# A two-block transformer on one core: row gathers of large expert units issued right behind their places, and two weight tiles of the first small experts loaded one step later

## The chip, the cores and the metric

The kernel runs on one core of a Trainium2 chip. The metric is the device time of one execution in microseconds (us); lower is better. The engines are named as in the profile: PE (matrix products; PEld its weight loads), DVE, ACT, POOL, and SP, which here only issues transfers. Transfers by DMA are started by SP (all weights) or by POOL (gathers of rows).

## The reference, cut to what matters

Four attention layers and a second block run first; the change lies in the last part, a mixture of experts over 256 tokens of width 1024 with 64 experts, 8 of which each token uses.

```python
def moe_ffn(h, w_router, e_bias, w_eg, w_eu, w_ed, w_sg, w_su, w_sd):
    ...
    gates = jnp.sum(jax.nn.one_hot(eidx, N_EXPERTS, dtype=jnp.float32) * w[..., None], axis=-2)
    ...
    def expert_chunk(args):
        xc, gch = args
        hg = jnp.einsum('cd,edf->cef', xc, w_eg)
        hu = jnp.einsum('cd,edf->cef', xc, w_eu)
        a = jax.nn.silu(hg) * hu * gch[..., None]
        return jnp.einsum('cef,efd->cd', a, w_ed)
    ...
    shared = (jax.nn.silu(t @ w_sg) * (t @ w_su)) @ w_sd
    return (routed + shared).reshape(B, S, D)
```

## The kernel before, in words

The kernel computes each expert only for the tokens that chose it. After routing, an expert with more than 64 tokens is a **large unit** (up to 128 tokens), two others share a step as a **small pair** (up to 64 tokens each). Units are numbered u = 0, 1, 2, ..., pairs p = 0, 1, .... `lone(u)` computes one large unit alone, for u = 0 to 4; then `both(5)`, `both(6)`, ... each compute one large unit and one small pair (pair p = u - 5), in a chain of branches that ends when the work does. `both(5)` is the first common step. From here on the order of instructions on each engine is the order in which the code is written; nothing is rescheduled.

A large unit needs three weight matrices (gate, up, down) of 1 MB each. SP loads them into the three raw buffers `eraw`, in halves or whole (`load(u, j, h)`); ACT rounds a half to its high part (`hi`, tile `ehi`) and DVE subtracts to get the low part (`lo`, tile `elo`). PE multiplies with high and low parts: `wide(u, a, 0)` gate, `wide(u, a, 1)` up, `down(u, hf)` down. A raw half can be loaded again only when `lo` has read it. A small pair needs six tiles of 1 MB, `pair0` to `pair5` (gate, up, down of both experts), and PE uses them without splitting (`wide_p`, `down_p`; tiles 4 and 5 are read by `down_p` at the end of a common step). `load_p(p, *js)` loads those tiles. The table `early` says in which lone unit which tiles of pair 0 are loaded.

The rows of a unit's tokens come by these steps. `onehot(u)` (on POOL, tile `pm`) and `onehot_p(p)` (POOL, tile `ps`) make 0/1 matrices of which token has which place. `places(u)` lets PE multiply them, and DVE copies the resulting token numbers to `ix` (L1896). `fetch(t, i)` (L1901, POOL) gathers 128 rows of 4 KB from `hrow` in device memory by those numbers, into `xr` for a large unit and into the single buffer `xrp` for a pair (numbers `ip`). `cols(u, j)` turns the rows on PE (L1908) and ACT and DVE split the result into `x` (L278, L279); `cols_p(j)` does the same for a pair without splitting. `cols(u + 1, ...)` runs in step u, so that a unit's rows must be there one step ahead.

In the kernel before, `fetch` of unit u + 1 stands at the start of step u, though `places(u + 1)` was written in step u - 1; between the two, on POOL, stand the one-hots at the end of step u - 1: `onehot(u + 3)`, and from lone(2) on those of a pair. The fetch of pair 0 stands at the start of lone(4).

Of the kernel before, what the change touches and what calls it, by code (L numbers as in the profile page):

```python
# [232 lines left out]
class Kernel:  # L233
# [1574 lines left out]
    def weights(self, col, j):  # L1808
        e = self.nc.sync.value_load(self.eid[0:1, col:col + 1], min_val=0, max_val=E - 1)
        return self.ins["w_exp"][bass.ds(e, 1), :, 2048 * j:2048 * j + 2048].rearrange("o p n -> p (o n)")  # L1810
# [6 lines left out]
    def load(self, u, j, h=None):  # L1817

        part = (lambda t: t) if h is None else lambda t: self.half(t, j, h)
        self.nc.sync.dma_start(part(self.eraw[j]), part(self.weights(u, j)))  # L1820
# [21 lines left out]
    def units(self, num, y):  # L1842
# [18 lines left out]
        xr = [mp.tile([P, D], F32, name=f"xr{i}") for i in range(2)]  # L1861
        xr_p = mp.tile([P, D], F32, name="xrp")
        self.yt = [xr[hf][:, tt * 512:(tt + 1) * 512] for hf in range(2) for tt in range(2)]
        ix, ix_p = [[mp.tile([P, 1], I32, name=f"{t}{i}") for i in range(2)] for t in ("ix", "ip")]
# [10 lines left out]
        def hi(j, h):  # L1875
            nc.scalar.activation(half(hl[0][j], j, h), half(raw[j], j, h), AF.Copy)  # L1876

        def lo(j, h):
            V.tensor_tensor(half(hl[1][j], j, h), half(raw[j], j, h), half(hl[0][j], j, h).bitcast(F32), OP.subtract)  # L1879
# [7 lines left out]
        def places(u):  # L1887

            t = pm[u // 2 % 2][:, :, u % 2]
            b = self.tbank()  # L1890
            for tt in range(2):
                nc.tensor.transpose(b[:, tt * P:(tt + 1) * P], t[:, tt].bitcast(F32), self.ident)
            for tt in range(2):
                nc.tensor.matmul(b[:, S:S + 4], t[:, tt], self.gsp[:, tt, u, :], start=(tt == 0), stop=(tt == 1))
            if u > 1:
                V.tensor_copy(ix[u % 2], b[:, S + 2:S + 3])  # L1896
            V.tensor_copy(pt[u % 4], b[:, :S])
            V.tensor_reduce(gc[u % 4], b[:, S:S + 2], AX.X, OP.add)

        def fetch(t, i):  # L1900
            nc.gpsimd.indirect_dma_start(out=t, out_offset=None, in_=self.hrow,  # L1901
                                         in_offset=bass.IndirectOffsetOnAxis(ap=i[:, :1], axis=0))
# [8 lines left out]
        def cols(u, j):  # L1911
            x = [t[:, 4 * j:4 * j + 4, (u % 2) * P:(u % 2 + 1) * P] for t in self.x]
            self.split(x[0], x[1], turned(xr[u % 2], j))

        def wide(u, a, c):
            ww = w(c, KT)
            for k in range(KT):
                x = [t[:, k, (u % 2) * P:(u % 2 + 1) * P] for t in self.x]
                for j, (q, p) in enumerate(((0, 0), (0, 1), (1, 0))):
                    nc.tensor.matmul(a[:, c * 256:(c + 1) * 256], x[p], ww[q][:, k, :],  # L1920
                                     start=(k == 0 and j == 0), stop=(k == KT - 1 and j == 2))

        def turn():
            b = self.tbank()
            for f in range(2):
                nc.tensor.transpose(b[:, f * P:(f + 1) * P], av[:, f * P:(f + 1) * P], self.ident)
            self.split(at[0], at[1], b[:, :S].rearrange("p (f t) -> p f t", f=2))
# [5 lines left out]
        def down(u, hf):  # L1933
            d = w(2, 2)
            a = self.abank()
            c = slice(512 * hf, 512 * hf + 512)
            for f in range(2):
                for j, (q, p) in enumerate(((0, 0), (0, 1), (1, 0))):
                    nc.tensor.matmul(a, at[p][:, f, :], d[q][:, f, c], start=(f == 0 and j == 0), stop=(f == 1 and j == 2))
            out(gc[u % 4], a, c)  # L1940

        def combine(t, hf):
            for tt in range(2):
                for p in range(2):
                    nc.tensor.matmul(y[tt][hf], t[:, tt * P:(tt + 1) * P], yo[p][:, 512 * hf:512 * hf + 512],  # L1945
                                     start=False, stop=False, skip_group_check=True)


        def load_p(p, *js):
            for j in js:  # L1950
                nc.sync.dma_start(R[j], weights(NB + 2 * p + j % 2, j // 2))
# [23 lines left out]
        def cols_p(j):  # L1975
            self.copy(xs[:, 4 * j:4 * j + 4, :], turned(xr_p, j), "va"[j])
# [21 lines left out]
                                     start=(f == 0), stop=(f == 1))  # L1998
            out(gc_p[p % 3], a, c)

        early = {1: (0,), 2: (1, 2), 3: (3,), 4: (4, 5)}

        def lone(u):


            if u:
                fetch(xr[(u + 1) % 2], ix[(u + 1) % 2])
            if u == L - 1:
                fetch(xr_p, ix_p[0])
            load(u + 1, 1, 0)  # L2010
            lo(1, 1)
            load(u + 1, 1, 1)
            if u:
                for h in range(2):
                    hi(2, h)
                    lo(2, h)
                    load(u, 2, h)
            load_p(0, *early.get(u, ()))
            a = self.abank()
            wide(u, a, 0)  # L2020
            if u:
                turn()
            else:
                places(2)
            if u > 1:
                combine(pt[(u - 2) % 4], 0)
            for h in range(2):
                hi(0, h)
                lo(0, h)
                load(u + 2, 0, h)  # L2030
            wide(u, a, 1)
            if u:
                cols(u + 1, 0)
            else:
                places(0)
            if u > 1:
                combine(pt[(u - 2) % 4], 1)
            nc.scalar.activation(sv, a[:, 0:256], AF.Silu)
            V.tensor_tensor(av, a[:, 256:512], sv, OP.mult)
            hi(1, 0)  # L2040
            if u:
                down(u - 1, 0)
                cols(u + 1, 1)
            places(u + 2 if u else 1)
            lo(1, 0)
            hi(1, 1)
            if u == L - 1:
                cols_p(0)
            if u:
                down(u - 1, 1)  # L2050
            if u == L - 1:
                cols_p(1)
            if u > L - 3:
                places_p(u - L + 2)
            onehot(u + 4)
            if u >= L - 3:
                onehot_p(u - L + 3)
# [8 lines left out]
        def both(u):  # L2066

            p = u - L
            fetch(xr[(u + 1) % 2], ix[(u + 1) % 2])
            fetch(xr_p, ix_p[(p + 1) % 2])  # L2070
            if not p:
                load(u + 1, 1, 0)
                lo(1, 1)
                load(u + 1, 1, 1)
                for h in range(2):
                    hi(2, h)
                    lo(2, h)
                    load(u, 2, h)
                turn()
                for hf in range(2):  # L2080
                    combine(pt[(u - 2) % 4], hf)
                for hf in range(2):
                    down(u - 1, hf)
            a = self.abank()
            wide(u, a, 0)
            if p:
                cut(u)
            nc.scalar.activation(sv, a[:, 0:256], AF.Silu)
            if not p:
                for hf in range(2):  # L2090
                    combine(pt[(u - 1) % 4], hf)
            places(u + 2)
            b = self.abank()
            wide_p(b, 0)
            load_p(p + 1, 0, 1)
            for h in range(2):
                hi(0, h)
                lo(0, h)
            load(u + 2, 0)
            cols(u + 1, 0)  # L2100
            nc.scalar.activation(sv_p, b[:, 0:256], AF.Silu)
            wide(u, a, 1)
            V.tensor_tensor(av, a[:, 256:512], sv, OP.mult)
            cols(u + 1, 1)
            if not p:
                cut(u)
            wide_p(b, 1, range(0, 4))
            turn()
            wide_p(b, 1, range(4, KT))
            load_p(p + 1, 2, 3)  # L2110
            V.tensor_tensor(av_p, b[:, 256:512], sv_p, OP.mult)
            hi(1, 0)
            lo(1, 0)
            down(u, 0)
            turn_p()
            hi(1, 1)
            lo(1, 1)
            load(u + 2, 1)
            down(u, 1)
            cols_p(0)  # L2120
            combine(pt[u % 4], 0)
            down_p(p, 0)
            combine(pt[u % 4], 1)
            down_p(p, 1)
            load_p(p + 1, 4, 5)
            cols_p(1)
            combine(pt_p[p % 3], 0)
            places_p(p + 2)
            combine(pt_p[p % 3], 1)
            onehot(u + 4)  # L2130
            onehot_p(p + 3)
# [74 lines left out]
```

## Time and profile before

| what | value |
|---|---|
| median of 3 runs | 1279.52 us (1278.63 to 1283.08) |
| the profiled execution's own time | 1282.81 us |
| its span, first to last instruction | 1280.9 us |
| mean granted PE clock | 0.977 of full speed |
| PE busy | 1206.8 us, 94% of the span |
| DVE, ACT, POOL busy | 960.9, 691.3, 239.1 us |
| transfers | 298.77 MB, mean 233 GB/s |

The span is 1.9 us shorter than the execution's own time, and that execution took 3.3 us more than the median. The work on the experts starts at about 892 us of the span. lone(0) runs to about 899 us; the first waiting matrix products of later steps are at 908 us in lone(1), 921 us in lone(2) and 935 us in lone(3); lone(4) runs from 940.5 us, both(5) from 956 us on, and the products end at about 1267 us. A row of a timeline gives start, duration, engine, line, operation, tiles written and read, shape and count, and in brackets how long the engine had been idle and what ended that.

### The profile page before, as it was taken

To read this page: it belongs to the slowest core of one execution; us is meant where nothing else is said; L and a number is where in the kernel's file an instruction comes from. 1 tells how busy PE (TensorE), PEld (TensorE's weight loads), DVE (VectorE), ACT (ScalarE), POOL (GpSimd) and SP (SyncE) were. 2 spreads that over 40 slices of the span, in tenths; PEclk is the share of its full clock that TensorE was granted. 3 is DMA by queue.
4 is the path that set the end of the run, shared out by engine and by line. 5 is a ranking of instruction groups with operands and counts; after the bars stand their busy time and mean duration, and the time that the engine had idled before them with its cause. 6 is when DMAs were issued, how large, how long until landed. Compare 5 with 4: busy or idle time off the path is not lost. (4 is left out here: it accounts for less than half of the span.)

```text
span 1280.9 us, 23092 instructions
## 1 busy us (share of the span) xinstructions
PE 1206.8 (94%) x8278; PEld 1021.1 (80%) x8278; DVE 960.9 (75%) x2395; ACT 691.3 (54%) x1508; POOL 239.1 (19%) x307
## 2 busy tenths in 40 slices
PE   5999998999989999999989999988889999999995
PEld 5887786998879987999879898777877777766773
DVE  6877889879987797878689679887884555555554
ACT  5667786446644564557755555543753443444431
POOL 2034521001100110001100000020551332222320
PEclk9988999999989999999999999999999999999998
DMA  7460314673357644777435225243998999999997
GB/s 292 150 258 13 111 43 148 246 264 130 107 197 272 231 150 167 264 265 261 172 141 181 100 95 197 101 170 136 370 401 307 400 380 388 388 398 385 375 391 284
DMA packets 50926, 298.77 MB, mean 233 GB/s; under 512 B 5776, under 2 KB 6576, under 8 KB 20848
## 3 DMA queue, kind: packets, MB, share of 16 engines
q1 hardware_dynamic: 42912, 271.94, 56.2%
q0 software_dynamic: 5728, 21.73, 4.8%
q10 hardware_dynamic: 2160, 3.52, 0.8%
q8 instruction: 67, 1.10, 0.4%
q14 instruction: 59, 0.48, 0.1%
HBM read 295.05 MB, written 2.11 MB: 232 GB/s over the span
## 5 line engine op out<-in xcount | busy, mean ns | idle before, releaser
L351 ACT ACTIVATE hi<-raw 128x512 fp32r<-128x512 f32 (+4 forms) x452 | 247.1, 604 | 128.2 <-PE acc L415 61.0
L358 DVE TENSOR_TENSOR lo<-raw,hi 128x512 fp32r<-128x512 f32 (+5 forms) x446 | 286.6, 670 | 27.7 <-ACT hi L351 26.7
L415 PE MATMUL acc<-x,hi 128*128 128x256 f32 x1440 | 278.3, 292 | 0.0
L415 PEld LDWEIGHTS acc<-x,hi 128*128 128x128 f32 x1440 | 229.1, 195 | 9.7 <-issue 7.9
L415 PE MATMUL acc<-x,lo 128*128 128x256 f32 x720 | 207.2, 288 | 3.1 <-DVE lo L358 3.1
L415 PEld LDWEIGHTS acc<-x,lo 128*128 128x128 f32 x720 | 140.1, 195 | 4.4 <-DVE lo L358 3.7
L1879 DVE TENSOR_TENSOR elo<-eraw,ehi 128x1024 fp32r<-128x1024 f32 x100 | 119.7, 1226 | 15.6 <-ACT ehi L1876 15.5
L453 PE MATMUL acc<-hi,x 128*128 128x256 f32 x544 | 108.5, 296 | 4.4 <-DVE x L279 1.9
L1876 ACT ACTIVATE ehi<-eraw 128x1024 fp32r<-128x1024 f32 x100 | 102.4, 1054 | 12.5 <-DMA eraw<-in_w_exp_dram 12.3
L1920 PE MATMUL acc<-ehi,x 128*128 128x256 f32 x512 | 94.8, 285 | 1.3 <-ACT x L273 1.3
L453 PEld LDWEIGHTS acc<-hi,x 128*128 128x128 f32 x544 | 89.9, 200 | 7.1 <-DVE x L279 3.0
L1982 PE MATMUL acc<-pair,xs 128*64 128x256 f32 x704 | 83.3, 384 | 0.0
L1920 PEld LDWEIGHTS acc<-ehi,x 128*128 128x128 f32 x512 | 80.4, 191 | 3.6 <-ACT x L273 1.5
L453 PE MATMUL acc<-lo,x 128*128 128x256 f32 x272 | 79.2, 292 | 0.3 <-DVE lo L358 0.3
L642 ACT ACTIVATE p<-sb,m 128x256 f32<-128x256 f32 (+1 forms) x136 | 61.2, 452 | 30.6 <-DVE m L641 26.0
L1920 PE MATMUL acc<-elo,x 128*128 128x256 f32 x256 | 72.6, 284 | 0.7 <-DVE elo L1879 0.7
L387 DVE SCALAR_TENSOR_TENSOR macc<-raw,sc,macc 128x512 f32<-128x512 f32 x84 | 63.5, 756 | 8.5 <-DMA raw<-in_w_all_dram 6.9
L278 ACT ACTIVATE x<-t 128x512 fp32r<-128x512 f32 x50 | 29.6, 596 | 70.5 <-PE t L1908 57.2
L1982 PEld LDWEIGHTS acc<-pair,xs 128*64 128x64 f32 x704 | 47.7, 137 | 24.4 <-issue 3.7
L583 PE MATMUL acc<-hi,g 128*128 128x512 f32 x192 | 63.1, 400 | 0.0
L1901 POOL DMA_INDIRECT xrp<-hrow,ip x12 | 19.9, 1659 | 200.8 <-PE o L1945 196.0
L453 PEld LDWEIGHTS acc<-lo,x 128*128 128x128 f32 x272 | 54.3, 200 | 0.5 <-DVE lo L358 0.5
(589 smaller groups left out, 2644.9 us busy)
## 6 DMA issues: line engine op xcount, KB each, us to landing
raw<-in_w_all_dram SPq DMA_DIRECT2D x128, 1024.0 KB, 4.8
pair<-in_w_exp_dram SPq DMA_DIRECT2D x72, 1024.0 KB, 8.0
eraw<-in_w_exp_dram SPq DMA_DIRECT2D x33, 1024.0 KB, 8.5
eraw<-in_w_exp_dram SPq DMA_DIRECT2D x40, 512.0 KB, 6.7
gain<-in_rows_dram POOLq DMA_DIRECT2D x8, 512.0 KB, 4.0
raw<-in_w_all_dram SPq DMA_DIRECT2D x2, 832.0 KB, 4.5
nab<-in_na_bias_dram POOLq DMA_DIRECT2D x1, 1536.0 KB, 7.1
h<-in_x_dram SPq DMA_DIRECT2D x2, 512.0 KB, 10.4
```

The lines of the kernel that those rows point to most:

```text
L278: self.cut = self.nc.scalar.activation(hi, src, AF.Copy)
L351: self.nc.scalar.activation(hi[:, c], raw[:, c], AF.Copy)
L358: eng.tensor_tensor(lo[:, c], raw[:, c], hi[:, c].bitcast(F32), OP.subtract)
L387: nc.vector.scalar_tensor_tensor(self.macc, w[:, k, :], sc, self.macc, op0=OP.mult, op1=OP.add)
L415: self.nc.tensor.matmul(av[:, i, :], w[:, k, c], x[u][:, k, :], start=(k == 0 and j == 0), stop=(k == nk - 1 and j == 2))
L453: self.nc.tensor.matmul(a[:, :n], self.x[u][:, k, tt * P:(tt + 1) * P], ww[:, k, :], start=(k == 0 and j == 0), stop=(k == KT - 1 and j == 2))
L583: self.nc.tensor.matmul(a, gt[u][:, 4 * i + k, tt * P:(tt + 1) * P], ww[:, k, :], start=(i == 0 and k == 0 and j == 0), stop=(i == 1 and k ...
L642: nc.scalar.activation(out, sb[:, :n], AF.Exp, bias=m, scale=-1.0, accum_out=ssum)
L1876: nc.scalar.activation(half(hl[0][j], j, h), half(raw[j], j, h), AF.Copy)
L1879: V.tensor_tensor(half(hl[1][j], j, h), half(raw[j], j, h), half(hl[0][j], j, h).bitcast(F32), OP.subtract)
L1920: nc.tensor.matmul(a[:, c * 256:(c + 1) * 256], x[p], ww[q][:, k, :], start=(k == 0 and j == 0), stop=(k == KT - 1 and j == 2))
L1982: nc.tensor.matmul(a[64 * e:64 * e + 64, c * 256:(c + 1) * 256], xs[:, k, 64 * e:64 * e + 64], t[e][:, k, :], start=(k == 0), stop=(k == K ...
```

## The change

In `places(u)`, for u > 1, the gather of the unit's rows is now issued as soon as DVE has been given the copy of the token numbers; the two fetches of large units at the start of `lone` and `both` are gone. Unit 2 is therefore fetched in lone(0), units 3 to 6 in lone(1) to lone(4), and every common step u fetches unit u + 2 in place of u + 1. Pair fetches stay where they were. The table `early` gives one tile of pair 0 to each of lone(1) to lone(4), and tiles 4 and 5 are loaded in both(5), behind the reload of the down weights. There is one gather more in all.

```diff
@@ -1896,6 +1896,8 @@
                 V.tensor_copy(ix[u % 2], b[:, S + 2:S + 3])
             V.tensor_copy(pt[u % 4], b[:, :S])
             V.tensor_reduce(gc[u % 4], b[:, S:S + 2], AX.X, OP.add)
+            if u > 1:
+                fetch(xr[u % 2], ix[u % 2])
...
-        early = {1: (0,), 2: (1, 2), 3: (3,), 4: (4, 5)}
+        early = {1: (0,), 2: (1,), 3: (2,), 4: (3,)}
 
         def lone(u):
 
 
-            if u:
-                fetch(xr[(u + 1) % 2], ix[(u + 1) % 2])
             if u == L - 1:
                 fetch(xr_p, ix_p[0])
             load(u + 1, 1, 0)
@@ -2066,7 +2066,6 @@
         def both(u):
 
             p = u - L
-            fetch(xr[(u + 1) % 2], ix[(u + 1) % 2])
             fetch(xr_p, ix_p[(p + 1) % 2])
             if not p:
                 load(u + 1, 1, 0)
@@ -2076,6 +2075,7 @@
                     hi(2, h)
                     lo(2, h)
                     load(u, 2, h)
+                load_p(0, 4, 5)
                 turn()
```

On POOL the order before, from lone(2) to the start of both(5), is this: `xr_10799` and `xr_10800` are the two buffers of large units (here units 4, 5, 6), `pm` the one-hots of units 6, 7, 8, `ps` those of pairs 0, 1, 2.

```order
129 L1825 TENSOR_SCALAR pm<-consts_e,place 128x128 x2
130 L1957 TENSOR_SCALAR ps_10310<-consts_e,place 128x64 x4
131 L1901 DMA xr_10799<-hrow,ix_10802 128x1024
132 L1825 TENSOR_SCALAR pm<-consts_e,place 128x128 x2
133 L1957 TENSOR_SCALAR ps_10311<-consts_e,place 128x64 x4
134 L1901 DMA xr_10800<-hrow,ix_10803 128x1024
135 L1901 DMA xrp<-hrow,ip_10804 128x1024
136 L1825 TENSOR_SCALAR pm<-consts_e,place 128x128 x2
137 L1957 TENSOR_SCALAR ps_10310<-consts_e,place 128x64 x4
138 L1901 DMA xr_10799<-hrow,ix_10802 128x1024
```

After the change the same stretch of POOL reads as follows (the lines of the new file are two higher).

```order
129 L1903 DMA xr_10799<-hrow,ix_10802 128x1024
130 L1825 TENSOR_SCALAR pm<-consts_e,place 128x128 x2
131 L1959 TENSOR_SCALAR ps_10310<-consts_e,place 128x64 x4
132 L1903 DMA xr_10800<-hrow,ix_10803 128x1024
133 L1825 TENSOR_SCALAR pm<-consts_e,place 128x128 x2
134 L1959 TENSOR_SCALAR ps_10311<-consts_e,place 128x64 x4
135 L1903 DMA xrp<-hrow,ip_10804 128x1024
136 L1903 DMA xr_10799<-hrow,ix_10802 128x1024
```

The gather of unit 5 has moved ahead of the six one-hots of unit 7 and pair 1, and the gather of pair 0 (`xrp`, `ip_10804`), which stood right behind it, now stands behind those six one-hots.

On SP this is the piece of lone(4), behind the reload of the halves of unit 4's down weights; each load is preceded by the reading of an expert's number.

```order
 L1809 ISA x2
-L1951 ISA
-L1951 DMA pair_10778<-in_w_exp_dram 128x2048
-L1809 TENSOR_LOAD eid
-L1809 ISA x2
-L1951 ISA
-L1951 DMA pair_10779<-in_w_exp_dram 128x2048
+L1953 ISA
+L1953 DMA pair_10777<-in_w_exp_dram 128x2048
```

Two tiles of pair 0 (`pair_10778`, `pair_10779`, its tiles 4 and 5) have left lone(4), and one tile (3) has come; those two now stand in both(5). In lone(2) two tiles have become one in the same way.

## Rows read from the trace of the kernel before

**Rows 1.** Windows: PE, PEld, DVE, ACT, POOL busy us, PE clock, DMA share, GB/s.
```profile
920.00:940.00 20.00, 17.30 (x110) 15.14 (x110) 14.96 (x23) 13.88 (x19) 7.86 (x9) 1.00 1.03 408
960.00:964.00 4.00, 3.21 (x8) 2.59 (x9) 0.73 (x2) 0.61 (x1) 3.04 (x6) 0.57 1.02 403
968.00:972.00 4.00, 4.00 (x31) 3.00 (x31) 1.71 (x5) 2.28 (x3) 1.02 (x1) 1.00 0.03 9
1020.00:1040.00 20.00, 20.00 (x155) 15.77 (x154) 10.80 (x21) 8.80 (x14) 7.72 (x8) 1.00 0.97 373
```

**Rows 2.** Waits, 880 to 980 us: who waited for whom, total us, times, longest us.
```profile
POOL xr L1901 <- DVE ix L1896: 28.2, 5, 7.7
PE t L1908 <- DMA xr<-hrow,ix: 4.1, 3, 1.6
```

**Rows 3.** Timeline of PE: rows turned, first products of both(5), use of pair tiles.
```profile
908.12 0.66 PE L1908 MATMUL t<-consts,xr 128*128 128x128 f32 x4 [1.26 <-DMA xr<-hrow,ix]
...
921.10 0.66 PE L1908 MATMUL t<-consts,xr 128*128 128x128 f32 x4 [1.21 <-DMA xr<-hrow,ix]
...
934.83 0.66 PE L1908 MATMUL t<-consts,xr 128*128 128x128 f32 x4 [1.61 <-DMA xr<-hrow,ix]
...
952.62 0.66 PE L1908 MATMUL t<-consts,xrp 128*128 128x128 f32 x4 [1.45 <-DVE ix L1896]
...
960.79 0.79 PE L1939 MATMUL acc<-ehi,at 128*128 128x512 f32 x1 [2.18 <-DVE at L279]
...
986.44 1.94 PE L1997 MATMUL acc<-pair,ats 128*64 128x512 f32 x8
```

**Rows 4.** Timeline of POOL: gathers (L1901) and one-hots (L1825 units, L1957 pairs).
```profile
902.10 1.07 POOL L1901 DMA_INDIRECT xr<-hrow,ix  x1 [0.17 <-DVE gc L1898]
...
915.94 5.35 POOL L1957 TENSOR_SCALAR ps<-consts_e,place 128x64 fp32r<-128x64 f32 x4
926.58 1.02 POOL L1901 DMA_INDIRECT xr<-hrow,ix  x1 [5.29 <-DVE ix L1896]
927.62 1.28 POOL L1825 TENSOR_SCALAR pm<-consts_e,place 128x128 fp32r<-128x128 f32 x2
928.89 4.29 POOL L1957 TENSOR_SCALAR ps<-consts_e,place 128x64 fp32r<-128x64 f32 x4
940.32 1.02 POOL L1901 DMA_INDIRECT xr<-hrow,ix  x1 [7.14 <-DVE ix L1896]
942.81 0.93 POOL L1901 DMA_INDIRECT xrp<-hrow,ip  x1 [1.47 <-DVE ip L1971]
...
1001.28 1.02 POOL L1901 DMA_INDIRECT xr<-hrow,ix  x1 [0.15 <-issue]
```

**Rows 5.** Timeline of DVE: token numbers, second split of rows, low parts.
```profile
895.88 0.16 DVE L1896 CAST ix<-t 128x1 int32<-128x1 f32 x1 [0.17 <-PE t L1894]
...
909.94 0.68 DVE L279 TENSOR_TENSOR x<-t,x 128x512 fp32r<-128x512 f32 x1
...
928.42 3.63 DVE L1879 TENSOR_TENSOR elo<-eraw,ehi 128x1024 fp32r<-128x1024 f32 x3
...
951.88 0.68 DVE L279 TENSOR_TENSOR x<-t,x 128x512 fp32r<-128x512 f32 x1
```

**Rows 6.** Tile xr, windows 912:925, 925:938, 939:948: gathers from issue to landing.
```profile
DMA to landing us min/median/max: 7.4/7.4/7.4
...
DMA to landing us min/median/max: 8.2/8.2/8.2
...
DMA to landing us min/median/max: 6.3/6.3/6.3
```

**Rows 7.** Timeline of ACT: first high part that lone(3) makes.
```profile
932.88 1.06 ACT L1876 ACTIVATE ehi<-eraw 128x1024 fp32r<-128x1024 f32 x1 [3.04 <-DMA eraw<-in_w_exp_dram]
```

**Rows 8.** Timeline of SP's queue: last unit loads and first pair loads in both(5).
```profile
958.25 3.18 SPq L1820 DMA_DIRECT2D eraw<-in_w_exp_dram  x3
...
973.88 1.53 SPq L1951 DMA_DIRECT2D pair<-in_w_exp_dram  x2
```

## The prediction

> **What bounds the kernel now.** I read the windows first, to see where PE idles at all. From 1020 us on it does not: 20.00 us of work in 20, at a DMA share of 0.97 [rows 1]. The common steps are bound by PE. Earlier rows can win nothing there, and a slower POOL loses nothing as long as its gathers land in time. In the lone units PE works 17.30 us of 20 while the transfers are saturated, share 1.03 at 408 GB/s [rows 1]; whatever the change is worth is decided in that stage.
>
> The waits of the stage come next. PE waited for gathered rows three times, 4.1 us in all [rows 2], and the timeline says where: 1.26 us before 908.12, 1.21 before 921.10 and 1.61 before 934.83 [rows 3]. But POOL waited 28.2 us in five gathers for the token numbers `ix` [rows 2]; at 926.58 and 940.32 the gather started within 0.3 us of them [rows 4]. So those gathers already go out when their places are known, and moving them up in the program cannot start them earlier. Only the first one was held by the order: its numbers were there at 895.88 + 0.16 [rows 5], it started at 902.10 [rows 4].
>
> The largest later stalls have another cause. PE waited 1.45 us before 952.62, where the first rows of pair 0 are turned, and 2.18 us before 960.79 [rows 3]. The first ended when DVE had read the bank of products needed next: its split at 951.88 lasts 0.68, to 952.56 [rows 5]. The second waits for `at`, behind DVE's low parts. No transfer ends either.
>
> **The change part by part.** *The gather of unit 2* moves some 6 us forward, to about 896.3. Its 1.26 us wait goes. But in lone(1) the next place where PE meets DVE is the split at 909.94 [rows 5], which stands behind low parts that this change does not shorten. PE turns the rows sooner and then waits for that split. I take 0, between -1.3 us (the whole wait) and +0.4: the gather's 0.52 MB now passes while unit 1's halves arrive, 1.3 us of transfer at 408 GB/s, of which I let a third reach DVE.
>
> *The wait of 1.21 us in lone(2)*: with the first gather out of the way, the loads behind it arrive sooner, and ACT and DVE reach `ix` of unit 3 a little earlier. I take -0.8, between 0 and -1.2.
>
> *The wait of 1.61 us in lone(3)*: now one pair tile and not two lies on SP's queue in lone(2). The gather that met the two tiles took 8.2 us, the one before it, with a single tile, 7.4 [rows 6], so 0.8 us is the least. ACT's wait of 3.04 us for the next gate half [rows 7] shrinks as well, by up to the 2.6 us that 1.05 MB take at 408 GB/s. I take -1.4, between -0.8 and -1.6. The three together give -2.2, between -0.8 and -4.1.
>
> *Tiles 4 and 5 of pair 0* move past six loads of SP. They will be issued behind the load that ends at 958.25 + 3.18 = 961.4, and SP issues nothing more until 973.88 [rows 8]; the transfers stand still in between, share 0.03 from 968 to 972 [rows 1]. Even 10 us of landing puts them there by 974, and they are first read at 986.44 [rows 3]. This costs 0; without that hole they would push the next pair loads back by 5 us, which still leaves 7 us.
>
> *The gather of pair 0* is the hidden cost. It was second on POOL behind the gather of unit 5: 942.81 after 940.32 [rows 4]. Unit 5's gather is now written a step earlier, ahead of the one-hots of unit 7 and pair 1, but pair 0's has stayed at the start of lone(4), behind them. The gather of unit 5 cannot start sooner than its numbers, so the one-hots run between the two. How long that takes is seen one step earlier, where the same sequence stands: gather 926.58, one-hots 927.62 and 928.89, end at 933.18, 6.6 us after the gather began; with the 5.35 us seen at 915.94 it is 7.7 [rows 4]. I take 7.1. Landing takes between 6.3 and 8.2 [rows 6]; I take 7.0, since one pair tile will be in the queue. The rows land 14.1 us after 940.32 in the old clock. PE was held for other reasons until 952.62, 12.3 us after it [rows 3, 4]. The new stall is +1.8, between +0.6 and +3.6. Nothing takes it up: the work of `down` behind it on PE feeds ACT and DVE, and DVE's `at`, for which PE waits before 960.79, stands behind these.
>
> The one-hots were stretched by DVE. The 4.29 us at 928.89 [rows 4] overlap DVE's low parts, 928.42 to 932.05 [rows 5], and still ended only 1.1 us after them. The Trainium skill, "SBUF — State Buffer", section "Who interferes with whom", says that a DVE instruction with two SBUF inputs takes the read port that GpSimd shares, and that the loser blocks for the whole instruction. Taken strictly, the one-hots would begin only at 932.05, 3.2 us later, and my +1.8 would become up to +5.0; the trace does not agree with so full a block.
>
> *The clock.* The 2.18 us of idleness before 960.79 came with a granted clock of 0.57 of full speed from 960 to 964, the lower level of 1.2 GHz for most of that stretch [rows 1, 3]; 1.61 us before 934.83 came with none, 1.00 from 920 to 940. The stall before the pair's rows would grow from 1.45 to 3.3 us. A drop like the other would run the products behind it at half speed; the 3.21 us of PE work in those 4 us would fit in about half. I take +0.8, between 0 and +1.5.
>
> *The common steps.* There the gather at 1001.28 followed the one-hots and not its numbers [rows 4]; it now goes ahead of them. PE never idles there, so 0. One gather more is issued in the last step, 25 us before the products end, and nothing reads it: 0.
>
> **The sum**: -2.2 + 1.8 + 0.8 = +0.4 us on the profiled execution, 1282.81 to 1283.2. That execution lies 3.3 us above the median; on the median the forecast is 1279.52 + 0.4 = **1279.9 us**.
>
> **The rivals.** *No payback.* If the queue is so much emptier in lone(4) that pair 0's rows land within 12.3 us of the gather of unit 5, the gain stays: -2.2, at best -4.1, so 1277.3 down to 1275.4. For it: two pair tiles less by then. Against it: with 6.6 us of one-hots they would have to land in 5.7 us, and none of the three gathers of rows 6 did.
>
> *Slower: the pair's gather decides.* If the one-hots take 7.7 us and landing 8.2, the stall is +3.6; with the full clock term and only the least gain it is +3.6 + 1.5 - 0.8 = +4.3, 1283.8. It decides as soon as the rows land over 14.5 us after unit 5's gather began (stall equal to my gain). For it: the two gathers that met pair tiles took 7.4 and 8.2.
>
> *The queue's depth does not matter.* If a gather's landing hangs on how its packets alternate with SP's, and not on how many wait there, unit 4 gains nothing from the missing tile: the gain is only the -0.8 of lone(2), and the sum +1.8, 1281.3. For it: 6.3 us at 940.32, when the queue was as full as before. The Trainium skill, "DMA: Bandwidth & Descriptors", section "Queues, rings and completion order", says so: each transfer engine goes round robin between the queues, packet by packet.
>
> *The stage is bound by bytes.* At share 1.03 two tiles less are 2.10 MB, 5.1 us at 408 GB/s: 1274.4, if nothing else takes the place of the transfers. Against it: only 4.1 us of PE's waits in the stage were for gathered rows [rows 2].
>
> **How the numbers follow.** About 0.5% (6.4 us) is what a measurement of this kernel can tell from no change. Chances: the forecast, within about 1.5 us of 1279.9, 0.43; no payback 0.24; queue's depth 0.13; slower 0.13; bytes 0.05; something not seen here 0.02. No case reaches 6.4 us by itself: faster than 1273.1 needs the bytes case with the idle before 952.62 gone too, slower than 1285.9 the slower case with a loss in lone(1). I give faster 0.03, same 0.93, slower 0.04. The range is from 1276.2, inside the no-payback case, to 1283.2, inside the slower one; the tails beyond hold the bytes case and the ends of those two.
>
> **What would show it.** In the profile after: the first gather at 896 to 897 us; PE's waits for `xr` in lone(2) and lone(3) under 0.6 us each; POOL's one-hots of unit 7 and pair 1 between the gathers of unit 5 and of pair 0, which start 6.6 to 7.7 us apart; PE waiting for the landing of `xrp`, 2.5 to 4 us, with a second stretch of low clock behind it; a window near 968 us in which the transfers no longer stand still; common steps of the old length. The prediction is wrong if PE does not wait for `xrp`, if PE meets a wait for tiles 4 and 5, or if the common steps change.

## The result: PE waited 5 us longer for the pair's rows, and the kernel got slower

The changed kernel took 1287.01 us in the median (four executions, 1286.38 to 1289.98) against 1279.40 us before: ratio 1.0058, interval 1.0034 to 1.0083. That is 7.6 us slower, more than the 6.4 us that the prediction took for the least that a measurement of this kernel can tell from no change, and outside the forecast range of 1276.2 to 1283.2 us. The later runs of changed kernels had six to twelve executions each, beside new ones of the kernel before, and in the last experiment the difference turned out smaller: the changed kernel again took 1284.20 us against 1282.35 us, ratio 1.0024 (1.0007 to 1.0041). Put on the first time of before, that ratio is 1282.5 us and would lie inside the range. That the kernel is slower stands, since both intervals lie above 1; how much in the median lies between about 2 and 8 us.

The profiled execution of the changed kernel took 1286.85 us, span 1284.8 us. The windows show where PE now idles (columns as in [rows 1]):

```profile
920.00:940.00 20.00, 19.32 (x130) 17.18 (x129) 17.12 (x30) 15.44 (x21) 11.21 (x11) 1.00 1.02 395
940.00:944.00 4.00, 4.00 (x32) 3.82 (x31) 4.00 (x6) 2.28 (x3) 4.00 (x4) 1.00 0.93 342
944.00:948.00 4.00, 4.00 (x28) 3.50 (x26) 3.16 (x4) 2.18 (x4) 3.46 (x2) 1.00 0.87 278
948.00:952.00 4.00, 0.32 (x4) 0.23 (x2) 2.94 (x6) 1.76 (x3) 1.93 (x3) 0.89 1.00 411
952.00:956.00 4.00, 1.05 (x5) 1.08 (x6) 0.00 (x0) 0.00 (x0) 2.03 (x5) 0.50 1.02 416
956.00:960.00 4.00, 3.51 (x18) 2.86 (x17) 1.57 (x5) 1.61 (x3) 0.00 (x0) 0.76 0.31 124
...
964.00:968.00 4.00, 3.54 (x9) 2.79 (x10) 0.86 (x3) 0.69 (x1) 0.00 (x0) 0.60 1.00 358
968.00:972.00 4.00, 4.00 (x30) 3.76 (x29) 1.05 (x2) 0.94 (x2) 0.00 (x0) 0.98 1.04 409
1020.00:1040.00 20.00, 20.00 (x153) 14.57 (x152) 9.77 (x18) 8.15 (x12) 7.34 (x8) 1.00 0.97 372
```

From 1020 to 1040 us PE is full as before, and so it is from 940 to 948 us. From 948 to 956 us it worked 1.37 us of 8, and its clock fell to 0.50. The waits from 880 to 980 us, and the timeline of PE, name the reason; they answer to [rows 2, 3]:

```profile
PE t L1910 <- DMA xrp<-hrow,ip: 6.6, 1, 6.6
PE t L1910 <- DMA xr<-hrow,ix: 1.8, 2, 1.1
```

```profile
890.46 0.51 PE L1922 MATMUL acc<-ehi,x 128*128 128x256 f32 x2 [1.29 <-ACT x L273]
909.12 0.44 PE L1892 MATMUL t<-consts,pm 128*128 128x128 f32 x2 [1.01 <-DVE x L279]
919.19 0.66 PE L1910 MATMUL t<-consts,xr 128*128 128x128 f32 x4 [1.12 <-DMA xr<-hrow,ix]
931.96 0.66 PE L1910 MATMUL t<-consts,xr 128*128 128x128 f32 x4 [0.63 <-DMA xr<-hrow,ix]
954.95 1.09 PE L1910 MATMUL t<-consts,xrp 128*128 128x128 f32 x4 [6.63 <-DMA xrp<-hrow,ip]
964.46 0.56 PE L1941 MATMUL acc<-ehi,at 128*128 128x512 f32 x1 [2.19 <-DVE at L279]
973.84 2.38 PE L1984 MATMUL acc<-pair,xs 128*64 128x256 f32 x20
990.10 1.94 PE L1999 MATMUL acc<-pair,ats 128*64 128x512 f32 x8
```

The waits for large units' rows fell from 4.1 to 1.8 us, as they should. The wait for the pair's rows, 1.45 us before [rows 3], became 6.63 us, and a transfer ends it now. The timeline of POOL, which answers to [rows 4], shows why that transfer is late:

```profile
894.48 1.06 POOL L1903 DMA_INDIRECT xr<-hrow,ix  x1 [27.94 <-DMA eraw<-in_w_exp_dram]
...
937.45 1.00 POOL L1903 DMA_INDIRECT xr<-hrow,ix  x1 [4.06 <-DVE ix L1896]
938.48 1.29 POOL L1825 TENSOR_SCALAR pm<-consts_e,place 128x128 fp32r<-128x128 f32 x2
939.75 6.70 POOL L1959 TENSOR_SCALAR ps<-consts_e,place 128x64 fp32r<-128x64 f32 x4
946.61 1.00 POOL L1903 DMA_INDIRECT xrp<-hrow,ip  x1
```

The gather of unit 5 starts at 937.45, the six one-hots fill POOL until 946.45, and the gather of pair 0 starts at 946.61, 9.16 us after unit 5's. Before it was 2.49 us [rows 4]. It lands 8.2 us later.

The length of the stage is best read as distances between rows of PE, since the work on the experts starts at 892.32 us in one profile and 890.46 in another. A is the first product of lone(0), B the first product that turns the pair's rows, C the first pair product of both(5). All kernels that ran are in the table, so that each experiment can point to it; "gap" is the distance of the starts of the gathers of unit 5 and pair 0, "wait" PE's idle time before B.

| kernel | gap | wait | A to B | B to C | A to C | ratio to before (interval) |
|---|---|---|---|---|---|---|
| before | 2.49 | 1.45 | 60.30 | 17.56 | 77.86 | 1 |
| before, second profile | 2.49 | 1.45 | 59.68 | 16.45 | 76.13 | 1 |
| changed | 9.16 | 6.63 | 64.49 | 18.89 | 83.38 | 1.0058 (1.0034 to 1.0083) |
| changed, again | 9.16 | 6.89 | 62.86 | 18.08 | 80.94 | 1.0024 (1.0007 to 1.0041) |
| pair's gather first | 2.49 | 1.45 | 57.48 | 16.47 | 73.95 | 0.9981 (0.9962 to 0.9999) |
| gathers moved only | 9.16 | 7.40 | 66.23 | 18.20 | 84.43 | 1.0059 (1.0036 to 1.0082) |
| tiles moved only | 2.49 | 1.45 | 59.57 | 17.56 | 77.13 | 0.9977 (0.9961 to 0.9992) |
| one-hots twice | 10.80 | 7.67 | 63.79 | 19.07 | 82.86 | 1.0035 (1.0015 to 1.0055) |
| one-hots a step earlier | 2.50 | 1.45 | 57.97 | 17.56 | 75.53 | 0.9990 (0.9968 to 1.0011) |
| tiles one step later still | 2.50 | 1.45 | 58.59 | 17.52 | 76.11 | 0.9982 (0.9958 to 1.0006) |
| one-hots on DVE | 2.50 | 1.45 | 58.84 | 17.55 | 76.39 | 0.9995 (0.9971 to 1.0020) |
| unit 5's gather moved only | 9.17 | 7.82 | 68.71 | 18.81 | 87.52 | 1.0043 (1.0023 to 1.0063) |
| unit 2's gather moved only | 2.49 | 1.45 | 60.56 | 16.47 | 77.03 | 0.9992 (0.9970 to 1.0013) |

The distance from C to the first pair product of both(6) is 27.22 to 27.24 us in every one of them, and from C to the end of the last product it is 295.70 to 295.72 us (that end is at 1265.89 us in the first profile of before). So no kernel changed the common steps. A lies anywhere between 886.3 and 894.8 us, though no edit touches what stands ahead of it: much of the scatter of the whole times arises there, and A to C is the cleaner measure. It is 80.94 to 87.52 us in the five profiles with the late gather and 73.95 to 77.86 in the eight others.

### The profile page after: what moved, and what is told of

Its sections match the earlier page's. It is cut to its first block, busy times and chain, and to the rows that moved or that the text cites. A ratio compares the mean times of both kernels' runs of the same rounds, so it can differ in the third digit from the quotient of the medians.

```text
span 1284.8 us, 23091 instructions
## 1 busy us (share of the span) xinstructions
PE 1206.8 (94%) x8278; PEld 1021.3 (79%) x8278; DVE 962.0 (75%) x2395; ACT 691.4 (54%) x1508; POOL 231.0 (18%) x308
```

## The experiments

The theory after the result (A): the whole loss is that one order on POOL, six one-hots between two gathers. Rivals: the moved weight tiles delay the landing of the pair's rows (B), or the early first gather disturbs lone(1) (C).

**The pair's gather ahead of the one-hots** (all other parts of the change kept):

```diff
-            if u == L - 1:
-                fetch(xr_p, ix_p[0])
...
+            if u == L - 2:
+                fetch(xr_p, ix_p[0])
```

The added lines stand behind the pair's places in lone(3), ahead of the one-hots. Expected:

> The changed kernel, but the gather of pair 0 is issued in lone(3) right behind its places, ahead of the one-hots of unit 7 and pair 1. Theory A (the loss is this one gather: it starts 9.2 us after the gather of unit 5, lands 8.2 us later and holds PE 6.6 us, 5.2 more than the 1.45 of before, and the low clock behind it costs about 1.3): the wait for its landing goes, PE waits 1.4 to 1.5 us there for DVE as before, and the time is that of before less the 1 us gained in lone(2) and lone(3): 1278.4, 1277 to 1279.5. Theory B (the two tiles moved into both(5) cost it): nothing changes, 1286 to 1288. Theory C (the first gather, now among unit 1's loads, costs it): 1286 to 1288 as well.

Measured: 1279.23 us against 1281.68, ratio 0.9981. The order of POOL's rows, and the wait that is left:

```profile
932.77 1.00 POOL L1903 DMA_INDIRECT xr<-hrow,ix  x1 [4.09 <-DVE ix L1896]
935.26 0.97 POOL L1903 DMA_INDIRECT xrp<-hrow,ip  x1 [1.50 <-DVE ip L1973]
936.26 3.21 POOL L1825 TENSOR_SCALAR pm<-consts_e,place 128x128 fp32r<-128x128 f32 x2
939.45 3.62 POOL L1959 TENSOR_SCALAR ps<-consts_e,place 128x64 fp32r<-128x64 f32 x4
```

```profile
945.10 0.66 PE L1910 MATMUL t<-consts,xrp 128*128 128x128 f32 x4 [1.45 <-DVE x L279]
...
953.25 0.50 PE L1941 MATMUL acc<-ehi,at 128*128 128x512 f32 x1 [2.18 <-DVE at L279]
```

The one-hots still take 6.8 us, but now nothing waits for them; PE waits for DVE, as before. The loss is gone; a small gain may be left, since the interval reaches to 0.9999.

**The gathers moved only** (the table `early` and the loads of tiles as before):

```diff
-        early = {1: (0,), 2: (1,), 3: (2,), 4: (3,)}
+        early = {1: (0,), 2: (1, 2), 3: (3,), 4: (4, 5)}
...
-                load_p(0, 4, 5)
```

> The gathers as in the changed kernel, the table of early tiles as before (tiles 4 and 5 in lone(4)). Theory A: the stall before the rows of pair 0 stays at 5 us or grows a little, since the transfers are fuller; 1286 to 1289. Theory B: no loss, 1278 to 1280. Theory C: 1286 to 1288, with the loss in lone(1).

Measured: 1.0059, a wait of 7.40 us. The loss does not need the moved tiles; B falls.

**The tiles moved only** (the gathers where they were before):

```diff
-            if u > 1:
-                fetch(xr[u % 2], ix[u % 2])
...
+            if u:
+                fetch(xr[(u + 1) % 2], ix[(u + 1) % 2])
```

The second piece stands at the start of `lone`; the same fetch, without the condition, is back in `both`. Expected:

> The table of early tiles as in the changed kernel, the gathers as before. Theory A: a small gain from the shorter queue, 1278 to 1279 (PE's waits in lone(2) and lone(3) shrink by 0.1 to 1 us together). Theory B: 1285 to 1287. Theory C: as A.

Measured: 0.9977 (1278.36 us against 1281.68). By itself this part gains some 3 us, more than the expected waits account for, and PE meets no wait for tiles 4 and 5. PE's wait for rows in lone(3) is gone in its profile, but the stage of 77.13 us lies between the two of before, so one profile does not show where the 3 us come from.

**The one-hots of pair 1 made twice in lone(3)** (the doubled cost):

```diff
+            if u == L - 2:
+                onehot_p(1)
```

> The changed kernel with the four one-hots of pair 1 written a second time in lone(3), behind the first (the same values). Theory A: four instructions more stand ahead of the gather of pair 0, 0.43 us each when DVE makes no low part and 2.2 to 2.5 when it does; DVE's low parts end when the first four end, so about 1.8 us; PE waits 8.4 us instead of 6.6, and the time is 1288.8, 1288 to 1290.5. Theories B and C: 1286.5 to 1287.5, as the changed kernel.

```profile
938.59 0.99 POOL L1903 DMA_INDIRECT xr<-hrow,ix  x1 [4.03 <-DVE ix L1896]
939.62 1.29 POOL L1825 TENSOR_SCALAR pm<-consts_e,place 128x128 fp32r<-128x128 f32 x2
940.90 8.34 POOL L1959 TENSOR_SCALAR ps<-consts_e,place 128x64 fp32r<-128x64 f32 x8
949.39 1.00 POOL L1903 DMA_INDIRECT xrp<-hrow,ip  x1 [0.15 <-issue]
```

The gap grew by 1.64 us to 10.80, near the 1.8 expected. PE's wait grew to 7.67 us only, not to 8.4, since this gather landed after 7.6 us and not 8.2, and the time of 1286.80 us missed the expected 1288 to 1290.5. The ratio of 1.0035 does not separate it from the changed kernel (1.0058 and 1.0024): a microsecond more is less than the scatter. The gap supports A, the time is inconclusive. The second four one-hots took 1.64 us more, 0.41 each, the first four 6.70. What differs is their neighbour on DVE: its last low part had ended at 947.36 us, before the second four began.

**The one-hots of pair 1 a step earlier**, in lone(2), so that only unit 7's two stand between the gathers:

```diff
-            if u >= L - 3:
-                onehot_p(u - L + 3)
+            if u == L - 3:
+                onehot_p(0)
+                onehot_p(1)
+            if u == L - 1:
+                onehot_p(2)
```

> The changed kernel, with one edit: the one-hots of pair 1 are made in lone(2), behind those of pair 0, and no longer in lone(3). The two gathers keep their places in the code. Only the two one-hots of unit 7 then stand on POOL between the gather of unit 5 and that of pair 0. Theory A (the pair's gather is late because POOL must first make six one-hots): the second gather starts about 2.5 us after the first instead of 9.2, PE's wait for the pair's rows goes from 6.63 us back to what DVE leaves, 1.5 to 2.2 us, and the ratio to the kernel before is 0.998 (0.996 to 1.0005), as it was with the gather written ahead of the one-hots. Theory B (the moved weight tiles make the pair's rows land late or the stage slow) leaves the ratio at 1.004 or above, since the loads are those of the changed kernel. A third outcome, 1.001 to 1.003: the four one-hots, now behind those of unit 6, hold the gather of unit 5 or DVE's low parts in lone(2) and cost there what they save.

Measured: gap 2.50, wait 1.45, ratio 0.9990. Both gathers stand in the code where the change put them, and the loss is gone. So it was the work between them.

**The same four one-hots made by DVE**:

```diff
-                onehot_p(u - L + 3)
+                onehot_p(u - L + 3, V if u == L - 2 else nc.gpsimd)
```

The engine is a second argument of `onehot_p` in this run.

> The changed kernel, with the four one-hots of pair 1 in lone(3) made by DVE instead of POOL; the order of the code is otherwise the same. Only the two one-hots of unit 7 then stand on POOL between the two gathers. On POOL these four took 0.43 us apiece alone and up to 2.5 us beside DVE's low parts. Theory A: the second gather starts about 2.5 us after the first, PE's wait for the pair's rows falls below 2.5 us; DVE pays about 4 x 0.25 us for them in a stage where its low parts are waited for, so the ratio is 0.998 to 1.000. If the loss were not in POOL's one-hots, the wait for the rows would stay at 6 us or more and the ratio at 1.005 to 1.007.

```profile
938.45 0.84 DVE L1959 TENSOR_SCALAR ps<-consts_e,place 128x64 fp32r<-128x64 f32 x4
939.10 3.49 DVE L1879 TENSOR_TENSOR elo<-eraw,ehi 128x1024 fp32r<-128x1024 f32 x3
```

Measured: gap 2.50, wait 1.45, ratio 0.9995. What cost POOL 6.70 us costs DVE 0.84.

**The tiles one step later still** (with the pair's gather first):

```diff
-        early = {1: (0,), 2: (1,), 3: (2,), 4: (3,)}
+        early = {2: (0,), 3: (1,), 4: (2,)}
...
-                load_p(0, 4, 5)
+                load_p(0, 3, 4, 5)
```

> The changed kernel with the gather of pair 0 written in lone(3) ahead of the one-hots, and the pair's weights moved on by one more tile: tile 0 in lone(2), 1 in lone(3), 2 in lone(4), tiles 3, 4 and 5 in both(5). If what is left of PE's waits for gathered rows in lone(2) and lone(3) (0.34 and 0.68 us with one tile in each step) comes from the tiles in SP's queue, both go to nearly nothing and the ratio to the kernel before is 0.9965 to 0.9985, up to 1.5 us better than with the pair's gather alone. If the waits hang on how the packets of a gather alternate with those of SP and not on how many wait there, nothing moves: 0.998. The rival on the other side: tile 3 (the up weights that pair 0 needs in the first half of both(5)) comes too late, PE waits for it, and the ratio is over 1.001.

Measured: 0.9982, nothing gained over the pair's gather first (0.9981), and nothing lost to tile 3. The time fits both of the first two expectations. The wait for rows in lone(2) went, but that in lone(3) was 1.24 us here and not near nothing, so neither of the two is borne out as a whole.

**One gather moved at a time**, in the kernel before: that of unit 5, or that of unit 2.

```diff
+            if u == 5:
+                fetch(xr[u % 2], ix[u % 2])
...
-            if u:
+            if u and u != 4:
```

For unit 2 the numbers are 2 and 1. Expected for unit 5, then for unit 2:

> The kernel before, with one gather moved: that of unit 5 stands in places(5), in lone(3), instead of at the start of lone(4). All other gathers and all weight tiles stay as in before. On POOL the six one-hots of unit 7 and pair 1 then stand between it and the gather of pair 0. Theory A (this one order is the whole loss): the two gathers start 9 us apart, PE waits 6 to 7.5 us for the pair's rows, the stage from the first product of lone(0) to the pair products of both(6) takes 109 to 112 us (103.4 and 105.1 in two profiles of before), and the ratio to before is 1.004 to 1.0075. A rival in which the loss needs the moved weight tiles or the other early gathers as well gives less than 1.003.

> The kernel before, with one gather moved: that of unit 2 stands in places(2), in lone(0), instead of at the start of lone(1). It starts about 6 us sooner and PE's wait for its rows in lone(1) (1.26 and 1.45 us in two profiles) goes. If PE then only waits for DVE's split of the rows, as the prediction has it, the time is that of before within its scatter, 0.9985 to 1.0015. If the time is kept, 1.3 us or more, the ratio is 0.9975 to 0.999; a gain over that can't come from this wait alone.

Unit 5's gather alone gives the full wait, 7.82 us, and 1.0043, with every other gather and every tile where it was. That is theory A in its smallest form. The wait and the stage, 87.52 us from A to C and 114.75 to both(6), are longer than expected (7.5 and 112 at most): the gather of the pair took 9.5 us to land here, and PE waited 2.82 us for unit 2's rows in lone(1), ahead of the place of the edit, against 1.26 and 1.45 in the two profiles of before. Unit 2's alone gives 0.9992, no change; in its profile PE turns the rows without waiting and then waits for DVE's split instead:

```profile
912.73 0.44 PE L1892 MATMUL t<-consts,pm 128*128 128x128 f32 x2 [1.00 <-DVE x L279]
```

C falls with it.

**Both kernels once more.** Expected for the kernel before, then for the changed one:

> The kernel before, unchanged, for one more profile. The profiled execution of before took 1282.81 us, 3.3 us over its median; the changed kernel's profiled execution is at its median. If the 3.3 us are pieces of low clock that fall elsewhere in the program from one execution to the next, this profile shows the same stage from lone(0) to both(6), 105 us within 1 us, and the difference in other places. If the stage itself varies, its length is another: 102 us or less would say that the first profile overstated the stage.

> The changed kernel once more, in as many executions as the experiments have, and for a second profile. The kernel with the one-hots of pair 1 made twice came out at 1.0035 where over 1.0058 was expected. If the changed kernel itself lies at 1.004 to 1.005 in more executions, that difference is scatter; if it stays at 1.006 or above, the doubled one-hots cost nothing or gain, which the theory doesn't explain. In the profile: the gathers of unit 5 and pair 0 9 to 9.5 us apart, PE's wait for the pair's rows 6 to 7.5 us, the stage 109.5 to 111.5 us.

The second profile of before (1283.80 us) has a stage of 76.13 us from A to C against 77.86, and the changed kernel's second 80.94 against 83.38: the stage itself varies by about 2 us from one execution to the next, more than the 1 us I expected, so single profiles are good to that and no better. To both(6) the second profiles have 103.37 us, between the two cases that I had named, and 108.17 us, below the 109.5 to 111.5 expected; the gap of 9.16 us and the wait of 6.89 are as expected. In all four pairings the changed kernel's is longer, by 3.1 to 7.3 us. Twelve executions of the changed kernel reached 1282.04 to 1290.03 us, against 1275.04 to 1287.37 of before, ratio 1.0024. That is below both cases that I had named, 1.004 to 1.005 and 1.006 or above. So the first ratio, from four executions each, was at the high end, and the run with the one-hots twice (1.0035) no longer lies below the changed kernel.

## Why the prediction was wrong

**The step that failed is the size of the stall before the pair's rows**: +1.8 us forecast, +0.6 to +3.6 allowed, +5.2 measured (6.63 - 1.45; +5.4 in the second profile). The mechanism was the one forecast: unit 5's gather cannot start before its numbers, the six one-hots run between, the pair's rows land too late. Both of its terms were too small:

- one-hots: 7.1 us from gather to gather forecast, 7.7 at most; measured 9.16 in both profiles of the changed kernel, 9.16 and 9.17 in two other kernels.
- landing: 7.0 us forecast, 6.3 to 8.2 allowed; 8.2 measured, and PE starts 8.34 after the issue. This was at the end of its bounds. The late gather of pair 0 took 7.6 to 9.5 us to land in the five profiles that have it, the early one 5.7 to 7.3 in the eight others; what slows it was not tried.

Together 17.50 us from unit 5's gather to the turned rows; minus the 12.30 of before is 5.20.

The first term was read from the wrong row. I took the same six one-hots at 927.62 and 928.89 [rows 4], a step earlier. There DVE had three low parts to make [rows 5] and then stopped for want of input, 1.59 us before the row at 933.97. Behind unit 5's gather it has five. The trace of before shows both, in DVE's timeline up to and just behind unit 5's numbers:

```profile
933.97 1.23 DVE L1879 TENSOR_TENSOR elo<-eraw,ehi 128x1024 fp32r<-128x1024 f32 x1 [1.59 <-ACT ehi L1876]
...
939.90 0.15 DVE L1896 CAST ix<-t 128x1 int32<-128x1 f32 x1
...
942.97 3.58 DVE L1879 TENSOR_TENSOR elo<-eraw,ehi 128x1024 fp32r<-128x1024 f32 x3
...
946.81 2.35 DVE L1879 TENSOR_TENSOR elo<-eraw,ehi 128x1024 fp32r<-128x1024 f32 x2
```

In before, six one-hots already stood at this place, those of unit 8 and pair 2:

```profile
943.78 3.25 POOL L1825 TENSOR_SCALAR pm<-consts_e,place 128x128 fp32r<-128x128 f32 x2
947.01 3.60 POOL L1957 TENSOR_SCALAR ps<-consts_e,place 128x64 fp32r<-128x64 f32 x4
```

They took 6.8 us, and a gap worked out from them would have been 7.9 us: nearer, but still short of 9.16. There the one-hots start 0.8 us behind the first of the low parts. After the change the one-hots of unit 7 and pair 1 fall on these low parts. POOL's four one-hots of pair 1, one by one (four windows of its timeline), and DVE beside them:

```profile
939.75 0.43 POOL L1959 TENSOR_SCALAR ps<-consts_e,place 128x64 fp32r<-128x64 f32 x1
940.16 2.51 POOL L1959 TENSOR_SCALAR ps<-consts_e,place 128x64 fp32r<-128x64 f32 x1
942.65 1.28 POOL L1959 TENSOR_SCALAR ps<-consts_e,place 128x64 fp32r<-128x64 f32 x1
943.91 2.55 POOL L1959 TENSOR_SCALAR ps<-consts_e,place 128x64 fp32r<-128x64 f32 x1
```

```profile
940.10 3.53 DVE L1879 TENSOR_TENSOR elo<-eraw,ehi 128x1024 fp32r<-128x1024 f32 x3
943.55 0.41 DVE L279 TENSOR_TENSOR at<-t,at 128x256 fp32r<-128x256 f32 x1
943.88 2.34 DVE L1879 TENSOR_TENSOR elo<-eraw,ehi 128x1024 fp32r<-128x1024 f32 x2
```

The first, before the low parts begin, takes 0.43 us. The second ends at 942.67, two low parts (2.4 us) later, the third at 943.93, with the third low part, the fourth at 946.46, with the last two. Each of these three ends 0.2 to 0.3 us after a low part has ended, and the same four durations, within 0.01 us, stand in all five profiles with the late gather. The Trainium skill, "SBUF — State Buffer", section "Who interferes with whom", has it that a DVE instruction with two SBUF inputs and a GpSimd instruction that reads SBUF contend for a shared port, and that the later one blocks entirely. These rows agree in that one-hots are held back; that two of the three waited through more than one low part is taken up at the end. The prediction named the rule and set it aside because the row at 928.89 ended 1.1 us after three low parts. That row agrees too: two one-hots were held to 932.36, and two more took 0.43 each. The +5.0 that the prediction worked out beside the rule is close to what came, but in part by luck: it stands for a gap of 10.3 us and a landing of 7.0, where 9.16 and 8.34 were measured.

The rival **"the pair's gather decides"** is what happened. Its point of decision was right (over 14.5 us; it was 17.5) and its price for the stall, +3.6, too low for the same reason.

**The other terms came out near their forecasts, as far as the scatter lets one see.** The gains: without the added stall, A to B is 64.49 - 5.18 = 59.31 us, and 62.86 - 5.44 = 57.42 in the second profile. That is 0.4 to 2.9 us less than the 60.30 and 59.68 of before; -2.2 was forecast, between -0.8 and -4.1. The stage scatters by as much, so this bears out the direction and not the size. With the loss removed in three ways the ratios are 0.9981, 0.9990 and 0.9995, 2.4 to 0.6 us faster, of which only the first interval leaves out 1. *Unit 2's gather*: it starts 4.0 us after A (894.48 - 890.46), as worked out, and 0 was forecast; 0.9992 by itself, and the wait moved to DVE's split as described. *lone(2)*: forecast 0.4 us of wait left; 1.12 and 0.77. *lone(3)*: forecast 0.2 left; 0.63, and none in the second profile. Here the missing tile does matter, as the forecast had it and the rival not: with two tiles loaded in lone(2) unit 4's gather lands after 8.1 to 8.4 us and the wait is 1.5 to 1.8 us in five profiles (1.61, 1.60, 1.54, 1.52, 1.78); with tile 1 alone the landing is 6.5 to 7.3 us and the wait 0 to 0.68 in seven. Whether the depth of the queue does it or the bytes that go ahead is not told apart, and with tile 0 in that place the landing was 7.9 us and the wait 1.24, which stays unexplained. *Tiles 4 and 5*: 0 forecast, no wait; the window from 968 us, in which the transfers had stood still [rows 1], now has a share of 1.04, as forecast, while that from 956 us fell to 0.31. *Common steps*: unchanged (27.23 us from C to both(6) in all four profiles, within 0.01).

**The clock**: +0.8 forecast, between 0 and +1.5; B to C grew by 1.3 us, and by 0.5 in the second profile, both against the first profile of before. Against its second, in which the stage is at full clock, it grew by 2.4 and 1.6 us. The size held against the first, its reason only in part. B to C is 16.45 to 16.47 us at full clock (three profiles), 17.5 to 17.6 with one piece at 1.2 GHz (five), 18.1 to 19.1 in the five profiles where PE idled 6.6 to 7.8 us: the lower level came with the long idle each time. But the 2.2 us of idleness before `at`, which I took for the cause of the drop in [rows 1], brought none in the second profile of before, none with the pair's gather first and none with unit 2's gather moved alone. That part of the reason is not borne out.

In the sum, from the first profile to the first: -1.0 + 5.2 + 1.3 = +5.5 us from A to C (83.38 - 77.86), where +0.4 was forecast. The range missed because the bounds of the one-hots' term were taken from neighbouring rows with fewer low parts beside them. The medians differ by more than this stage at first (7.6 us) and by less in the last run (about 2 to 3 us); that rest is scatter elsewhere, and the second time alone would not have shown the error.

## What to carry to other kernels

When an operation moves ahead in an engine's queue, look at what now stands in front of the one that stayed: here one gather moved up for nothing, and the next, which mattered, fell behind six operations. Where a duration is borrowed from another place, check what the neighbouring engine does at the new place; for POOL reading SBUF beside DVE, count DVE's two-input operations there, and not the share of time that POOL looked busy elsewhere. A few tenths of a per cent need a dozen executions: four put the same change at 1.0058, twelve at 1.0024. The distance between two rows of one engine inside the stage shows such a change more clearly than the whole time does, as long as the work behind the stage keeps its length.

## What the hardware showed that was not expected

A waiting POOL one-hot did not always get its turn when DVE's instruction ended. The one at 940.16 waited through two low parts, the next through one, the last through two; the same 2.5, 1.28, 2.5 came in all five profiles with the late gather. The low parts lose nothing: three take 3.53 us here, and the median of one in the whole stage is 1.22 us before and after. Following each other, DVE's instructions overlap at their ends in the records (three times 1.22 is 3.66), and the waiting engine may be passed over there; this last is a guess from the times and was not tried by itself.
